# Sparse-attention trunk in split fp32: the key and value compression as split products on token windows, and another order of the attention layer's steps

## The chip, the cores and the metric

The kernel runs on one core of a Trainium2 chip as one launch. The metric is the device time of that launch in microseconds (us); lower is better. Times are medians over several runs. A profile of one further execution gives the trace from which all durations are read. PE is the matmul engine, ACT, DVE and POOL are the three element-wise engines, and SP issues the DMAs of the weights.

## The reference, cut to what matters

The program is a trunk of four layers over 256 tokens of width 1024, all in fp32. Layers 0 and 3 mix tokens by native sparse attention (NSA), layer 1 by block attention (MoBA), layer 2 by a gated convolution; a SwiGLU feed-forward part follows each. The change is in the two NSA layers. There, 16 heads in 4 groups attend in three ways (compressed, selected, window), and a gate weighs the three. What the change touches is the compression of keys and values:

```python
q, k_c, v_c, k_s, v_s, k_w, v_w, gates = jnp.split(h @ w_in, NSA_SPLITS, axis=-1)
n_cmp = (S_ - CMP_BLOCK) // CMP_STRIDE + 1                      # 15 blocks of 32 tokens, 16 apart
cmp_idx = jnp.arange(n_cmp)[:, None] * CMP_STRIDE + jnp.arange(CMP_BLOCK)[None, :]

def compress(kv, pos, w1, w2):
    blk = kv[:, cmp_idx] + pos[None, None, :, None, :]
    blk = jnp.moveaxis(blk, 3, 2).reshape(B_, n_cmp, G, CMP_BLOCK * dh)
    return jax.nn.gelu(blk @ w1) @ w2                            # w1: 2048 x 256, w2: 256 x 64

kc, vc = compress(k_c, pos_k, k_w1, k_w2), compress(v_c, pos_v, v_w1, v_w2)
s_cmp = jnp.einsum('bsgrd,bcgd->bgrsc', q, kc)
o = gates[0] * o_cmp + gates[1] * o_slc + gates[2] * o_win       # (schematic)
```

## The kernel before

**Numbers in halves.** Nearly every product is made of fp32r operands that are split: a high half (the value rounded to fp32r) and a low half (what is left). `mm3` multiplies high by high, high by low and low by high into the same PSUM bank (L200 to L202 when it is called from `group`).

**Weights.** All weights stand in DRAM as one stream of parts. A part is 128 x 1024 fp32 (512 KB), that is 8 tiles of 128 x 128, in the order in which the steps use them: the function `stream` walks the same list of steps. `take` hands out tiles and sees to it that the next five parts are being prepared (`AHEAD`). To prepare a part (`split_part`), SP loads it into a `raw` buffer (6 of them), ACT writes the high half `whi` (L170), and DVE, or POOL where the table `LO` says so, writes the low half `wlo = raw - whi` (L174); `whi` and `wlo` have 5 buffers each. The parts of step F are the exception: SP loads them straight into a `whi` buffer as plain fp32, named `wf`, and nothing is split.

**The NSA layer.** `NSA_ORDER` is a list written by hand; each letter is a step, and the steps' instructions are issued in that order on each engine, as far as a scheduler at build time doesn't interleave neighbours. The steps are:
- A: the raw keys and values for the compression, four projections; `put_raw` copies them, scaled by the row norm, to two tiles `xs`, with a token's place inside its block along the columns.
- K, q, G, V: projections of keys, of query pairs (8 of them), of the gates, and of the values. One of K, q or G is one weight part, 24 matmuls of 128 x 256; V is four parts, 48 matmuls of 128 x 512.
- F (four times, 8 weight parts): `compress`, the product with w1. Before, the weight tile is the stationary operand and a strided view of `xs` with 80 columns (64 blocks and one column for the position's part) the moving one; 64 fp32 matmuls in a layer, all into one PSUM bank (L808).
- E: `activate`, the tanh form of GELU over that bank (L815 on). C and D: the product with w2, for keys and values. c and t: scores and weights of the compressed attention. g: the gates, transposed (L765) and put through a sigmoid.
- s: the scores of one pair of heads (L941, L944) and its softmax: DVE scales and takes the maxima (L587), ACT the exponentials (L591), POOL multiplies by gate and sum (L595). T: transposes of the result (L960 to L962) and its split (ACT L259, DVE L260). P: the product with the values (L979, L984, L986).

After the last P comes the output projection (L220, L224), part of which fills gaps between the last steps. Among the pairs, a stage with little of s, T and P (here called the projection stage) is followed by one in which six of the eight pairs run one after another (the softmax stage).

## Time and profile before

| | before |
|---|---|
| median of 3 runs | 1235.78 us (1235.66 to 1240.07) |
| the profiled execution | 1236.7 us, of it 1234.9 us span |
| PE | 1211.9 us busy (98% of the span) |
| DVE | 959.7 us (78%) |
| ACT | 710.6 us (58%) |
| POOL | 283.2 us (23%) |

Layer 0's attention lies in the first 150 us of the span or so, layer 3's between about 900 and 1040 us. "Busy" is the sum over the records of an engine; matmul records overlap, since a matmul starts before the one ahead of it has ended, so the pace of matmuls is read from the distance of their starts. In the groups of instructions, a row gives source line, engine, operation, what is written from what, the shape, the count, then the busy time, the mean duration in ns, and the engine's idle time ahead with what ended it. In the chain of waits, a row is a start, a length and the work that held the end back.

### The profile page before, as it was taken

To read this page: it belongs to the slowest core of one execution; us is meant where nothing else is said; L and a number is where in the kernel's file an instruction comes from. 1 tells how busy PE (TensorE), PEld (TensorE's weight loads), DVE (VectorE), ACT (ScalarE), POOL (GpSimd) and SP (SyncE) were. 2 spreads that over 40 slices of the span, in tenths; PEclk is the share of its full clock that TensorE was granted. 3 is DMA by queue.
4 is the path that set the end of the run, shared out by engine and by line. 5 is a ranking of instruction groups with operands and counts; after the bars stand their busy time and mean duration, and the time that the engine had idled before them with its cause. 6 is when DMAs were issued, how large, how long until landed. Compare 5 with 4: busy or idle time off the path is not lost.

```text
span 1234.9 us, 19497 instructions
## 1 busy us (share of the span) xinstructions
PE 1211.9 (98%) x6740; PEld 1051.4 (85%) x6740; DVE 959.7 (78%) x1709; ACT 710.6 (58%) x1258; POOL 283.2 (23%) x405
## 2 busy tenths in 40 slices
PE   8999999999999999999999999999999999999997
PEld 8987888888899888888888888888899878888886
DVE  7578798885778797987769897895746787889753
ACT  5489756564456545764444555574435896566543
POOL 1067650010111542000113250000220676400000
PEclk9999999999999999999999999999999999999999
DMA  7773265657555545666765655675768522656671
GB/s 280 249 241 99 69 208 163 221 186 250 191 172 153 172 127 186 233 202 194 278 196 164 191 184 171 200 240 165 245 193 253 157 89 75 221 166 209 198 261 38
DMA packets 96450, 231.40 MB, mean 187 GB/s; under 512 B 18272, under 2 KB 43232, under 8 KB 96352
## 3 DMA queue, kind: packets, MB, share of 16 engines
q1 hardware_dynamic: 95920, 229.61, 57.9%
q8 instruction: 53, 0.87, 0.3%
q10 hardware_dynamic: 432, 0.56, 0.1%
q14 instruction: 45, 0.37, 0.1%
HBM read 213.33 MB, written 1.05 MB: 174 GB/s over the span
## 4 chain that ended last, share of the span: by engine, by line
PE 81%; DVE 7%; ACT 5%; DMA 3%; POOL 2%; issue 1%; SPq 0%; POOLq 0%; ACTq 0%; DVEq 0%
PE psA L220 13%; PE psA L224 7%; PE psA L472 5%; PE psA L470 5%; PE psA L471 5%; PE psB L471 3%; PE psB L472 3%; PE psB L470 3%; PE psA L200 2%; PE psA L202 2%; PE psA L201 2%; DVE wlo L174 2%; PE psB L220 2%; ACT pr L591 2%; PE psB L412 1%; PE psB L410 1%
## 5 line engine op out<-in xcount | busy, mean ns | idle before, releaser
L170 ACT CAST whi<-raw 128x1024 fp32r<-128x1024 f32 (+1 forms) x347 | 357.0, 1038 | 293.6 <-DMA raw<-in_w 54.5
L174 DVE TENSOR_TENSOR wlo<-raw,whi 128x1024 fp32r<-128x1024 f32 (+1 forms) x334 | 410.2, 1246 | 143.9 <-ACT whi L170 121.0
L220 PE MATMUL psA<-ff,whi 128*128 128x512 f32 x686 | 181.8, 392 | 0.1
L220 PEld LDWEIGHTS psA<-ff,whi 128*128 128x128 f32 x686 | 124.6, 189 | 22.8 <-DVE row L1021 0.6
L200 PE MATMUL psA<-at,whi 128*128 128x256 f32 x352 | 101.3, 288 | 1.2 <-DVE row L557 1.2
L595 POOL TENSOR_SCALAR pr<-pr,rc,gates 128x256 f32<-128x256 f32 (+1 forms) x128 | 74.3, 595 | 119.2 <-DVE rc L593 114.5
L224 PE MATMUL psA<-ff,wlo 128*128 128x256 f32 x686 | 101.0, 282 | 0.0
L224 PEld LDWEIGHTS psA<-ff,wlo 128*128 128x128 f32 x686 | 96.0, 191 | 5.4
L202 PE MATMUL psA<-at,wlo 128*128 128x256 f32 x352 | 99.8, 284 | 0.0
L472 PE MATMUL psA<-whi,at 128*128 128x512 f32 x256 | 99.6, 389 | 0.0
L470 PE MATMUL psA<-whi,at 128*128 128x512 f32 x256 | 99.6, 389 | 0.0
L471 PE MATMUL psA<-wlo,at 128*128 128x512 f32 x256 | 99.6, 389 | 0.0
L201 PE MATMUL psA<-at,whi 128*128 128x256 f32 x352 | 99.5, 283 | 0.0
L137 ACT CAST shi<-B 128x1024 fp32r<-128x1024 f32 x56 | 58.8, 1051 | 53.9 <-DVE B L123 21.0
L287 POOL TENSOR_TENSOR ssq<-ssq,row 128x256 f32<-128x256 f32 x42 | 34.1, 811 | 210.6 <-ACT row L285 153.4
L174 POOL TENSOR_TENSOR wlo<-raw,whi 128x256 fp32r<-128x256 f32 x96 | 69.6, 761 | 37.3 <-ACT whi L170 17.3
L138 DVE TENSOR_TENSOR slo<-B,shi 128x1024 fp32r<-128x1024 f32 x56 | 66.7, 1215 | 12.0 <-ACT shi L137 12.0
L471 PE MATMUL psB<-wlo,at 128*128 128x512 f32 x192 | 74.9, 390 | 0.5 <-DVE wlo L174 0.5
L470 PE MATMUL psB<-whi,at 128*128 128x512 f32 x192 | 75.2, 391 | 0.0
L472 PE MATMUL psB<-whi,at 128*128 128x512 f32 x192 | 74.8, 390 | 0.0
L591 ACT ACTIVATE pr<-pr,mn 128x256 f32<-128x256 f32 (+1 forms) x160 | 71.4, 448 | 2.1 <-DVE mn L587 1.4
L200 PEld LDWEIGHTS psA<-at,whi 128*128 128x128 f32 x352 | 67.3, 191 | 1.8 <-ACT whi L170 1.6
(283 smaller groups left out, 2674.3 us busy)
## 6 DMA issues: line engine op xcount, KB each, us to landing
raw<-in_w SPq DMA_DIRECT2D x352, 512.0 KB, 4.5
B<-in_w SPq DMA_DIRECT2D x32, 512.0 KB, 4.2
pt<-pt SPq DMA_DIRECT2D x320, 32.0 KB, 1.9
wf<-in_w SPq DMA_DIRECT2D x16, 512.0 KB, 4.8
keys<-keys SPq DMA_DIRECT2D x16, 128.0 KB, 2.5
ff<-row SPq DMA_DIRECT2D x32, 64.0 KB, 2.9
h<-in_xt SPq DMA_DIRECT2D x4, 256.0 KB, 4.7
raw<-in_w SPq DMA_DIRECT2D x4, 256.0 KB, 5.0
```

The costliest lines, as they stand in the source:

```text
L170: copy(hi[:, c], src[:, c])
L174: eng.tensor_tensor(out=lo[:, d], in0=src[:, d], in1=hi[:, d].bitcast(F32), op=OP.subtract)
L200: mm(out, wt[0], act[0], start=first, stop=False)
L201: mm(out, wt[0], act[1], start=False, stop=False)
L202: mm(out, wt[1], act[0], start=False, stop=last)
L220: mm(outs[o], w[0], acts[k].rearrange("p i s -> p (i s)"), start=(k == 0), stop=(k == n - 1))
L224: mm(outs[o][:, :S], w[1], acts[k][:, 0, :], start=False, stop=False)
L470: mm(o, a[:, 0, s], hi, start=(k == 0), stop=False)
L471: mm(o, a[:, 0, s], lo, start=False, stop=False)
L472: mm(o, a[:, 1, s], hi, start=False, stop=(k == KT - 1))
L591: nc.scalar.activation(pr[:, c], pr[:, c], AF.Exp, bias=mn[:, j:j + 1], scale=-1.0, accum_out=den[:, j:j + 1])
L595: getattr(nc, PR[j % len(PR)]).tensor_scalar(pr[:, c], pr[:, c], rc[:, j:j + 1], gates[j], op0=OP.mult, op1=OP.mult)
```

## The change

Two things change in the NSA layers; all else of the diff gives the same instructions as before (names of unused options, the unused steps O and o, the lists of engines that hold "p" throughout).

First, the order of steps. Second, the compression:
- The parts of F go the common way: `raw` by SP, high half on ACT, low half on DVE (`LO["F"] = "v"`).
- `put_raw` ends, for each of keys and values, in the new function `windows`: four casts of 128 x 256 on ACT and four subtractions of the same shape on DVE write the blocks' tokens as high and low halves side by side (for one place inside a block, 64 columns hold the high halves of 4 groups x 16 blocks, and the next 64 the low ones), and two small pairs of 128 x 16 put the position's part at the sixteenth block, which the compression doesn't use. A layer has twice that.
- `compress` makes these windows the stationary operand and 256 columns of `whi` or `wlo` the moving one: 64 fp32r matmuls of 128 x 256 in a layer into one bank of 512 columns. High and low tokens lie on different partitions of that bank.
- After the last F, ACT and DVE copy the bank's two halves to SBUF, and `activate` begins with 4 fp32 matmuls of 128 x 64 with `fold` (two identities above each other, made once), which add the two halves and turn the result into the layout of before.
- The memsets and copies of the position's part into `xs` go; POOL copies one column of it instead.

The core of the diff:

```diff
-NSA_ORDER = ("A K3 q q F F F K0 F E G g K2 q K1 q D C s c q s V t T q P s T q s P T q T c s s P P T s t P s T "
-             "P T T P P").split()
+NSA_ORDER = ("A G q K0 F q F K2 F F g E q C K1 q q s q c s t T V D s K3 T q P s T P s q T T s P c P s T t P s "
+             "P T T P P").split()
-LO = {"nsa_out": "p", "moba_out": "vp", "A": "p", "F": "ppv"}
+LO = {"nsa_out": "p", "moba_out": "vp", "A": "p", "F": "v"}
...
-        if self.names[q] == "F":
-            t = self.operands.tile([P, PART * P], F32, tag="whi", name=f"wf{q}", bufs=W_BUFS)
-            nc.sync.dma_start(t, self.ap["w"][q])
-            self.parts[x] = (t, t)
-            return
...
-        xs = [self.sb([P, 656], "pt", bufs=PT_BUFS) for _ in range(2)]
+        xs = [self.sb([P, 4, 8, 17], "pt", bufs=PT_BUFS) for _ in range(2)]
+        xw = [[], []]
         for a in range(2):
-            nc.gpsimd.memset(xs[a][:, 512:], 0.0)
-            x = xs[a][:, 512:640].rearrange("p (r c) -> p r c", c=16)
-            for i in range(2):
-                nc.vector.tensor_copy(x[:, :, i], pos[:, a, 8 * i:8 * i + 8])
+            nc.gpsimd.tensor_copy(xs[a][:, :, :, 16], pos[:, a, None, 8:].to_broadcast([P, 4, 8]))
...
+        def windows(a):
+            for hf in range(2):
+                for r in range(0, 8, 4):
+                    x = self.ff([P, 2, S]).rearrange("p i s -> p (i s)").rearrange("p (r i g c) -> p r i g c", r=4, i=2, g=4)
+                    src = xs[a][:, :, r:r + 4, hf:hf + 16].rearrange("p g r c -> p r g c")
+                    nc.scalar.copy(x[:, :, 0], src)
+                    nc.vector.tensor_tensor(out=x[:, :, 1], in0=src, in1=x[:, :, 0].bitcast(F32), op=OP.subtract)
+                    if hf == 0:
+                        src = pos[:, a, r:r + 4, None].to_broadcast([P, 4, 4])
+                        nc.scalar.copy(x[:, :, 0, :, 15], src)
+                        nc.vector.tensor_tensor(out=x[:, :, 1, :, 15], in0=src, in1=x[:, :, 0, :, 15].bitcast(F32),
+                                                op=OP.subtract)
+                    xw[a].append(x.rearrange("p r i g c -> p r (i g c)"))
...
             for jj in range(4 * n, 4 * n + 4):
-                w = self.take(4)[0]
-                for i in range(4):
-                    a, hf = divmod(i, 2)
-                    x = xs[a]
-                    src = bass.AP(tensor=x.tensor, offset=x.offset + jj % 8 * 16 + jj // 8,
-                                  ap=[list(x.ap[0]), [P, 5], [1, 16]])
-                    mm(pc[0][:, 2 * hf + a], w[:, i * P:(i + 1) * P], src, start=(jj == 0 and i == 0),
-                       stop=(jj == 15), skip_group_check=True)
+                hi, lo = self.take(4)
+                for i, w in enumerate((hi, lo)):
+                    for a in range(2):
+                        c = slice(a * S, (a + 1) * S)
+                        mm(pc[0][:, c], xw[a][jj // 4][:, jj % 4], w[:, c], start=(jj == 0 and i == 0 and a == 0),
+                           stop=(jj == 15 and i == 1), skip_group_check=True)
+            if n == 3:
+                halves = [self.row() for _ in range(2)]
+                nc.scalar.copy(halves[0], pc[0][:, :S])
+                nc.vector.tensor_copy(halves[1], pc[0][:, S:])
+                pc.append(halves)
...
+            ph = self.bank("B")
+            for a, x in enumerate(pc[1]):
+                for hf in range(2):
+                    o = (2 * hf + a) * DH
+                    mm(ph[:, o:o + DH], x[:, hf * P:(hf + 1) * P], self.fold, start=(a == 0 and hf == 0), stop=True,
+                       skip_group_check=True)
+            p4 = ph[:, :S].rearrange("p (n c) -> p n c", n=4)
```

What follows shows how this moves instructions. On DVE in layer 0, after the row norm `rb` has come, before; `row` is a projection scaled by the norm, `pt_15` and `pt_16` are the tiles `xs`, and `wlo13` is the low half of weight part 13 (the parts 7 to 12, 14 and 15 are F's and have none):

```order
L729 COPY pt_16_151<-row_39_374 64x128 x2
L729 COPY pt_16_151<-row_40_380 64x128 x2
L557 TENSOR_TENSOR row_41_386<-psA_34_330,rb_36_360 128x256
L557 TENSOR_TENSOR row_44_422<-psA_43_395,rb_36_360 128x256
L748 TENSOR_TENSOR keys_11_144<-row_41_386,keys_11_144 64x256
L748 TENSOR_TENSOR keys_12_145<-row_41_386,keys_12_145 64x256
L781 TENSOR_TENSOR row_45_425<-row_44_422,ff_42_394 128x256
L557 TENSOR_TENSOR row_48_457<-psA_47_430,rb_36_360 128x256
L781 TENSOR_TENSOR row_49_460<-row_48_457,ff_46_429 128x256
L174 TENSOR_TENSOR wlo13_488<-raw13_485,whi13_487 128x1024
L174 TENSOR_TENSOR wlo16_522<-raw16_519,whi16_521 128x1024
```

The same place of the changed program, where L758, L589, L820 and L180 are what L729, L557, L781 and L174 were, L770 and L774 are the windows' large and small subtractions, and `row_49` is the gates' projection:

```order
L758 COPY pt_16_153<-row_44_402 64x8x16 x2
L589 TENSOR_TENSOR row_49_424<-psA_34_332,rb_36_366 128x256
L180 TENSOR_TENSOR wlo9_431<-raw9_428,whi9_430 128x1024
L770 TENSOR_TENSOR ff_45_408<-pt_16_153,ff_45_408 128x4x64
L770 TENSOR_TENSOR ff_46_413<-pt_16_153,ff_46_413 128x4x64
L770 TENSOR_TENSOR ff_47_418<-pt_16_153,ff_47_418 128x4x64
L770 TENSOR_TENSOR ff_48_421<-pt_16_153,ff_48_421 128x4x64
L589 TENSOR_TENSOR row_52_458<-psA_51_427,rb_36_366 128x256
L774 TENSOR_TENSOR ff_45_408<-pos_14_150,ff_45_408 128x4x4
L774 TENSOR_TENSOR ff_46_413<-pos_14_150,ff_46_413 128x4x4
L180 TENSOR_TENSOR wlo10_469<-raw10_466,whi10_468 128x1024
L820 TENSOR_TENSOR row_53_460<-row_52_458,ff_50_426 128x256
```

Between the copies and the first low half that PE needs, DVE had only projections to scale and split; now the windows and the low halves of F's parts stand among them, in one queue.

On PE in layer 0, before, where step F is under way (`wf10`, `wf11` are F's parts, `whi13` and `wlo13` those of K0):

```order
L808 MATMUL psB_50_464<-pt_15_150,wf10_431 128x80 x2
L808 MATMUL psB_50_464<-pt_16_151,wf10_431 128x80 x2
L200 MATMUL psA_51_533<-at_1_118,whi13_487 128x256
L201 MATMUL psA_51_533<-at_1_118,whi13_487 128x256
L808 MATMUL psB_50_464<-pt_15_150,wf11_465 128x80 x2
L808 MATMUL psB_50_464<-pt_16_151,wf11_465 128x80 x2
```

In the changed program, where the first F matmul stands (L840; `ff_39` is a window, `whi9` and `wlo9` belong to the second q, `psB_65` receives the transposed gates):

```order
L207 MATMUL psA_58_534<-at_1_120,whi9_430 128x256
L840 MATMUL psB_56_504<-whi7_202,ff_39_380 128x256
L806 MATMUL psB_65_699<-ident_99,row_49_424 128x128 x2
L208 MATMUL psA_58_534<-at_1_120,wlo9_431 128x256
L206 MATMUL psA_58_534<-at_2_123,whi9_430 128x256
```

F's matmuls and the gates' transposes now stand in PE's queue ahead of a projection, and they read what DVE and ACT write.

On PE in layer 0, before, where the third pair's scores stand (L941 on `ff_61`; the product of the first pair, L979 and L984, is ahead of them):

```order
L202 MATMUL psA_132_1137<-at_8_139,wlo26_1008 128x256
L979 MATMUL psC_135_1178<-pt_128_1127,ff_116_1082 128x512 x2
L979 MATMUL psC_135_1178<-pt_129_1130,ff_118_1088 128x512 x2
L984 MATMUL psC_135_1178<-pt_130_1133,ff_120_1094 128x2x128 x2
L941 MATMUL psA_139_1197<-keys_10_143,ff_61_689 128x256 x4
L944 MATMUL psA_140_1198<-keys_10_143,ff_61_689 128x512 x2
```

The same scores in the changed program (L978 on `ff_70`; L602 to L604 end the values' projection, L892 is step D):

```order
L602 MATMUL psA_125_1106<-whi25_931,at_8_141 128x512
L603 MATMUL psA_125_1106<-wlo25_932,at_8_141 128x512
L604 MATMUL psA_125_1106<-whi25_931,at_8_141 128x512
L978 MATMUL psA_144_1207<-keys_10_145,ff_70_721 128x256 x2
L892 MATMUL psB_134_1179<-w2_13_148,row_135_1180 128x128 x2
L892 MATMUL psB_134_1179<-w2_13_148,row_136_1182 128x128 x2
L892 MATMUL psB_134_1179<-w2_13_148,row_137_1184 128x128 x2
L892 MATMUL psB_134_1179<-w2_13_148,row_138_1186 128x128 x2
L978 MATMUL psA_144_1207<-keys_10_145,ff_70_721 128x256 x2
L981 MATMUL psA_145_1208<-keys_10_145,ff_70_721 128x512 x2
```

The third scores come directly after V; the projection K3 and the first pair's product, which stood ahead of them, now stand behind.

More of the change, by code (lines that the diff above doesn't have):

```diff
@@ L153, in split_part @@
             return
-        if self.names[q] == "F":
-            t = self.operands.tile([P, PART * P], F32, tag="whi", name=f"wf{q}", bufs=W_BUFS)
-            nc.sync.dma_start(t, self.ap["w"][q])
-            self.parts[x] = (t, t)
+        lo_eng, hi_eng = (e.get(self.names[q], d) for e, d in ((LO, "v"), (HI, "a")))
+        lo_eng, hi_eng = (e[q % len(e)] if q >= 4 else d for e, d in ((lo_eng, "v"), (hi_eng, "a")))
+        if lo_eng == "d":
+            hi = self.wp.tile([P, PART * P], F32R, tag="raw", name=f"raw{q}", bufs=RAW_BUFS)
+            lo = self.operands.tile([P, PART * P], F32R, tag="wlo", name=f"wlo{q}", bufs=W_BUFS)
+            nc.gpsimd.dma_start(hi, self.ap["w"][q])
+            nc.scalar.activation(lo, hi.bitcast(F32), AF.Identity, scale=-1.0)
+            nc.gpsimd.dma_start(lo, self.ap["w"][q], accum_op=OP.add)
+            self.parts[x] = (hi, lo)
             return
@@ L331, in project, with open_column, feed_columns, high @@
         self.late = []
+    def open_column(self, acts):
+        self.columns.append([self.bank("A"), [self.take() for _ in range(KT)], 0])
+        self.feed_columns(acts[:-1])
+    def feed_columns(self, acts):
+        mm = self.nc.tensor.matmul
+        for col in self.columns:
+            o, ws, done = col
+            for k in range(done, len(acts)):
+                hi, lo = ws[k]
+                def high():
+                    mm(o, hi, acts[k].rearrange("p i s -> p (i s)"), start=(k == 0), stop=(k == KT - 1))
+                def low():
+                    mm(o[:, :S], lo, acts[k][:, 0, :], start=False, stop=False)
+                for f in (low, high) if k == KT - 1 else (high, low):
+                    f()
+            col[2] = max(done, len(acts))
     def out_proj(self, acts, norm):
         m = 0
-        for n in (4, 1, 1, 1, 1):
-            ps = [self.bank(OUT_BANKS[i]) for i in range(n)]
-            self.group_wide(ps, acts)
+        early, self.columns = self.columns, []
+        for n in ([-len(early)] if early else []) + [4] + [1] * (KT - 4 - len(early)):
+            if n < 0:
+                n = -n
+                self.columns = early
+                self.feed_columns(acts)
+                self.columns = []
+                ps = [c[0] for c in early]
+            else:
+                ps = [self.bank(OUT_BANKS[i]) for i in range(n)]
+                self.group_wide(ps, acts)
             for i, p in enumerate(ps):
@@ L385, in split @@
             def split():
-                with self.tc.issue_after(self.casts.ins), self.tc.issue_after(self.lows.ins):
+                with ExitStack() as behind:
+                    for i in self.latest:
+                        behind.enter_context(self.tc.issue_after(i.ins))
                     halves()
@@ L576, in values, with softmax @@
             put(t, p)
-    def softmax(self, cols, gates):
+    def softmax(self, cols, gates, by):
         nc = self.nc
@@ L650, in project_q @@
             q = self.ff([P, 2, S])
[L651 removed]
+            self.project([lambda x: self.split(q, self.scaled(x))], at)
             qs.append(q)
@@ L884, in compressed @@
             p3 = pc.rearrange("p (h c) -> p h c", c=16)
[L885 to L891 removed]
+            nc.vector.tensor_tensor(out=pc, in0=pq[:, :S], in1=self.cneg, op=OP.add)
             mx = self.sb([P, 16], "cmx")
@@ L1086, in run @@
         nc.vector.memset(self.ones, 1.0)
+        self.fold = const.tile([P, DH], F32, tag="fold", name="fold")
+        nc.gpsimd.tensor_tensor(out=self.fold, in0=self.ident[:, :DH], in1=self.ident[:, DH:], op=OP.add)
         warm = const.tile([P, 1], F32, tag="warm", name="warm")
@@ L1118, in stream @@
     r = lambda a, n: np.arange(a, a + n)
-    out = lambda w, j, step: [(step, w, j, r(0, 512))] + [(step, w, j, r(m * P, P)) for m in range(4, KT)]
+    out = lambda w, j, step, m=0: ([(step, w, j, r(m * P, 512))]
+                                   + [(step, w, j, r(i * P, P)) for i in range(m + 4, KT)])
     s = []
```

98 lines of the change are left out of this document (42 added, 56 removed).

## The prediction

> **What bounds the kernel now.** I began with the page's first part, which tells what each engine was busy with.
>
> ```profile
> span 1234.9 us, 19497 instructions
> ...
> PE 1211.9 (98%) x6740; PEld 1051.4 (85%) x6740; DVE 959.7 (78%) x1709; ACT 710.6 (58%) x1258; POOL 283.2 (23%) x405
> ```
>
> PE is the bound: matmul time that goes away is gained, unless PE then waits. So I cut layer 0's attention and layer 3's into stretches by the table of windows: start and end, length, then busy time (and instructions) of PE, PE's weight loads, DVE, ACT and POOL, the clock, and the share and rate of the DMAs.
>
> ```profile
> 24.00:50.00 26.00, 25.38 (x220) 25.18 (x220) 12.60 (x29) 10.81 (x20) 0.00 (x0) 1.00 0.69 233
> 50.00:86.00 36.00, 34.80 (x241) 31.71 (x240) 29.18 (x85) 26.47 (x62) 14.85 (x20) 1.00 0.77 254
> 86.00:142.00 56.00, 53.15 (x349) 45.45 (x348) 46.33 (x175) 51.18 (x154) 37.48 (x67) 1.00 0.28 83
> 908.00:940.00 32.00, 31.57 (x272) 31.32 (x271) 14.48 (x30) 11.50 (x21) 0.70 (x1) 1.00 0.71 229
> 940.00:960.00 20.00, 20.00 (x166) 19.83 (x166) 17.68 (x48) 14.85 (x34) 1.80 (x2) 1.00 0.82 238
> 960.00:1033.00 73.00, 69.71 (x440) 59.62 (x439) 57.66 (x214) 63.06 (x183) 49.22 (x84) 1.00 0.34 102
> ```
>
> Step F lies in the first row (layer 0) and the fourth (layer 3). There PE is full, and DVE and ACT are idle for more than half of the time. In the third and the last row, the softmax stage, ACT is busy for 91% and 86%, and PE has its idle time: 2.85 and 3.29 us. So the first place is PE's, the second nearly ACT's.
>
> Step F's price stands in the timeline of PE (start, length, what), and its count in the view of line 808:
>
> ```profile
> 921.72 0.28 PE L202 MATMUL psA<-at,wlo 128*128 128x256 f32 x1
> 921.84 9.17 PE L808 MATMUL psB<-pt,wf 128*128 128x80 f32 x80
> 930.81 0.36 PE L200 MATMUL psA<-at,whi 128*128 128x256 f32 x1
> ```
>
> ```profile
> L808 PEld LDWEIGHTS psB<-pt,wf x256: 186/192/193, 29.3 to 939.6; 128*128 128x128 f32 x128
> L808 PE MATMUL psB<-pt,wf x256: 234/274/338, 29.5 to 939.7; 128*128 128x80 f32 x128
> ```
>
> The 80 records from 921.84 to 930.81 come every 0.112 us, and the 128 x 256 matmul ahead of them took its 0.12 us from start to start. The 128 fp32 products of both layers left 256 records, two each: a layer's F costs 128 x 0.112 = 14.3 us.
>
> **F's matmuls.** Now 64 matmuls of 128 x 256 take 64 x 0.12 = 7.7 us, and the 4 fp32 products with `fold`, two records each at 0.112, 0.9 us. A layer's PE work falls by 14.3 - 7.7 - 0.9 = 5.7 us, both by 11.5. Were the new matmuls paced by their weight loads (0.192 us each) instead, F would cost 12.3 us and the gain fall to 1.1 a layer; I don't take it, because the old records, with the same loads, came every 0.112 us.
>
> [...]
>
> **What DVE and ACT get instead.** The prices are in the groups of DVE between 24 and 75 us, and of ACT between 60 and 142 us:
>
> ```profile
> L174 DVE TENSOR_TENSOR wlo<-raw,whi 128x1024 fp32r<-128x1024 f32 x12 | 14.7, 1226 | 9.2 <-ACT whi L170 9.1
> L557 DVE TENSOR_TENSOR row<-psA,rb 128x256 f32<-128x256 f32 x12 | 4.9, 420 | 2.4 <-PE psA L202 2.3
> L748 DVE TENSOR_TENSOR keys<-row,keys 64x256 fp32r<-64x256 f32 x8 | 3.3, 418 | 0.7 <-ACT keys L744 0.5
> L729 DVE COPY pt<-row 64x128 f32<-64x128 f32 x8 | 2.1, 263 | 0.1
> ```
>
> ```profile
> L170 ACT CAST whi<-raw 128x1024 fp32r<-128x1024 f32 x12 | 12.5, 1050 | 4.6 <-PE psA L572 2.0 <-DMA raw<-in_w 1.7 <-ACT ff L929 0.4
> ...
> L779 ACT CAST ff<-row 128x512 fp32r<-128x512 f32 x6 | 3.8, 627 | 1.8 <-DVE row L557 1.8
> L929 ACT ACTIVATE ff<-psA,rstd 128x256 fp32r<-128x256 f32 x8 | 3.7, 480 | 1.5 <-PE psA L572 1.1 <-DVE ff L931 0.4
> ...
> L861 ACT ACTIVATE ff<-gu,rsel 128x512 fp32r<-128x512 f32 x2 | 1.3, 720 | 0.0
> ...
> L744 ACT CAST keys<-row 64x256 fp32r<-64x256 f32 x2 | 0.8, 402 | 0.0
> ```
>
> A layer adds on DVE 8 low halves (9.8 us) and 8 window subtractions (3.4, priced as the 128 x 256 subtraction), and four small ones, for which no row is near: between 0 and 0.26, I take 0.16. That is 13.8 us. ACT gets 8 x 1.05 and 8 x 0.40, 11.6 us.
>
> **The F stretch becomes DVE's.** The new DVE queue from `rb` to the last F part's low half holds ten low halves (12.2), eight scaled projections (3.4), eight copies (2.1), eight windows (3.4), the small ones (0.6), two q and two key halves (1.7) and `rb` (0.4): 23.8 us; before, 10.1 lay between `rb` and the last low half of this stretch. These rows tell when `rb` starts in each layer and when the matmul behind F's last did:
>
> ```profile
> 23.91 0.44 DVE rb L312
> ```
>
> ```profile
> 916.30 0.43 DVE L312 COPY rb<-psB 128x256 f32<-128x256 f32 x1 [4.47 <-PE psB L310]
> ```
>
> ```profile
> 47.41 0.36 PE L200 MATMUL psA<-at,whi 128*128 128x256 f32 x1
> ...
> 90.87 0.63 PE L941 MATMUL psA<-keys,ff 128*128 128x256 f32 x4
> ...
> 141.38 1.17 PE L979 MATMUL psC<-pt,ff 128*128 128x512 f32 x4
> ...
> 939.73 0.36 PE L200 MATMUL psA<-at,whi 128*128 128x256 f32 x1
> ...
> 982.47 0.51 PE L941 MATMUL psA<-keys,ff 128*128 128x256 f32 x3
> ...
> 1032.80 1.17 PE L979 MATMUL psC<-pt,ff 128*128 128x512 f32 x4
> ```
>
> Layer 0: DVE writes F's last low half at 23.9 + 23.8 = 47.7 at the earliest, and PE ends F 0.7 later, at 48.4. By PE alone F would end at 47.4 - 0.6 (the stretch's idle time) - 6.6 (F without `fold`) + 2.9 (five projections stand ahead of F's end instead of four, 24 x 0.12) = 43.1. So PE waits 5.3 us, 4.7 more than before. These waits fall on the gates' transposes (they read a projection that DVE scales only after twelve copies and subtractions), on the first window and on the last low halves; behind them in PE's queue stand q, K2 and all of E. Layer 3: two of the low halves are made ahead of `rb`, so 21.4 us remain; 916.3 + 21.4 + 0.7 = 938.4 against 939.7 - 0.4 - 3.7 = 935.6, a wait of 2.8, 2.4 more. SP's loads of F wait for one of six `raw` buffers now instead of a free `whi`; I give them no price, since a buffer comes free with each low half, 1.2 us apart at best, and the DMAs were busy for 69% and 71% of the stretch.
>
> **The softmax stage starts earlier.** I follow the third pair's scores (L941 at 90.87 and 982.47). Ahead of them, PE loses F's 5.7, K3's 24 matmuls (2.9), the first pair's product (four 128 x 512 and two 128 x 256: 1.2) and D's eight (0.9): 10.7 us. In layer 0 a wait of 1.2 us on V's first projection goes as well:
>
> ```profile
> L200 PE MATMUL psA<-at,whi 128*128 128x256 f32 x48 | 13.9, 289 | 1.2 <-DVE row L557 1.2
> ```
>
> So the scores come at 90.9 - 10.7 + 4.7 - 1.2 = 83.7, 7.2 earlier, and in layer 3 at 982.5 - 10.7 + 2.4 = 974.2, 8.3 earlier. What moved behind them must be done there: on PE 5.2 us more, on ACT, which is the fuller, one weight part (1.05), K3's halves (0.8), two of D's copies (1.4) and two of V's (1.0) more, and one q less (0.6): 3.6 us. I count ACT's growth in full, because its share there is 91%. POOL's gate products keep their order, and the shifts of K3's and the q's rows, which SP issues, come where the DMAs are busy for 28%: no price. The last pair's product (L979 at 141.38 and 1032.80) comes 7.2 - 3.6 = 3.6 us earlier in layer 0 and 8.3 - 3.6 = 4.7 in layer 3. Behind it everything is as before. The sum is 8.3 us.
>
> Bounds: the waits in F could be none (7.1 us more gained) or twice as long (7.1 lost); ACT's growth could cost nothing (7.2 more) or bring three waits of the kind of V's in each layer (7.2 lost). Not all at once: the likeliest case spans 4 to 14 us. The other parts have one answer: four small casts, two copies of the bank's halves and POOL's column lie beside PE work; the unused options add nothing.
>
> The profiled execution took 1236.7, of it 1.8 outside the span, 0.9 above the median. 1236.7 - 8.3 - 0.9 gives 1227.5 us (own range 1222 to 1232).
>
> **Rivals.** *ACT keeps its idle time.* From the first scores to the last split, ACT's sum by these prices is the same in both orders, 69 us; ACT idles 9.5 us of the 36 in the second window, partly on V's matmuls. If V holds it up as long as before, the end moves only with the first scores. Ahead of these PE loses 5.3 us (F's 5.7, while C's 0.4 comes ahead of them), less the waits of 4.7 and 2.4: 0.6 and 2.9 us, 1232.3 in all. For it: V's 10.9 us stand in one piece still. Against: its idle time is there because T, q and P follow V before new scores come, and these now go elsewhere.
>
> *All of the work is gained.* DVE fills its idle time ahead of `rb`, PE loses no more in F than before, and the softmax stage gives up its idle 2.85 + 3.29 us: 11.5 + 6.1 = 17.6, 1218.2 us. Against: the sum of 23.8 us after `rb` can't begin before the projections are scaled.
>
> *Slower: DVE is held up by ACT's casts in the F stretch.* Low halves wait for the cast of their part: DVE's row says 9.1 us of idle time behind ACT's casts in 51 us. If 7.8 of these come on top of the 23.8 us, because casts queue behind the windows' casts and these behind DVE's scaling, each layer loses 7.8: 1227.5 + 15.6 = 1243.1. It decides from 4.2 us of such idle time a layer on, where the gain is gone. Against: ACT adds up to under half of the stretch, and today's idle time is that of a queue with nothing to do.
>
> *The halves don't pace at 0.12:* with the loads' 0.192, the gain falls by 4.6 a layer, to 1236.7.
>
> **Numbers.** Forecast 0.55; ACT's idle time 0.22; all gained 0.13; slower 0.07; pace 0.03. About 0.5%, 6.2 us, is what a measurement of this kernel can tell from no change: below 1229.6 counts as faster, above 1242.0 as slower. Of the forecast's range three quarters are faster: 0.41 + 0.13 = 0.54; slower 0.07 and 0.01 from the tails, 0.08; the rest is 0.38. The range runs from 1219 (most of "all gained" left out) to 1238 (slower left out).
>
> **What would show it.** Right: L840 every 0.12 us, 7.7 us a layer; DVE busy for over 90% from `rb` to F's end, at about 48 and 938 us; PE's idle time there on L806, L840 and low halves, 3 to 6 us; the third scores at about 84; ACT over 90% behind them. Wrong: F ending at 43 (DVE has room), ACT casts as DVE's releaser for over 4 us (the slower rival), or the third scores early and the last product not (ACT's idle time).

## The result, and the profile after the change

The changed kernel takes 1230.69 us (median of 6 runs, 1228.91 to 1232.4), the kernel before 1236.82 (6 runs, 1235.66 to 1240.07): a ratio of 0.9949, 95% interval 0.9934 to 0.9964. It is 6.1 us faster; 8.3 were forecast. In executions of the kernel before with a mean granted clock of 0.998 or more it took 1236 to 1239 us, in those with 0.996 or less 1240 to 1243, so its medians, and the ratios to it, depend on how many of either kind stand beside a run. The changed kernel's profiled execution took 1231.72, 1.0 above its median, with this first part of the page:

```profile
span 1229.9 us, 19380 instructions
...
PE 1202.0 (98%) x6628; PEld 1043.2 (85%) x6628; DVE 985.2 (80%) x1743; ACT 732.5 (60%) x1300; POOL 288.0 (23%) x406
```

PE is as full as before, with 9.9 us less busy time; DVE has 25.5 us more and ACT 21.9. The table of windows shows where the gain lies. The stretches of layer 0 are now cut at four events: the copy of `rb`, the end of step F, the third pair's scores and the last pair's product (layer 3 likewise; the fourth row runs from the last product to the next layer's `rb`). Before:

```profile
23.91:47.41 23.50, 22.88 (x201) 22.68 (x199) 10.37 (x25) 10.24 (x18) 0.00 (x0) 1.00 0.67 232
...
90.87:141.38 50.51, 47.74 (x311) 40.52 (x310) 42.99 (x167) 46.06 (x145) 33.33 (x61) 1.00 0.26 81
141.38:351.63 210.25, 210.03 (x1051) 178.63 (x1051) 168.44 (x219) 113.64 (x152) 38.25 (x46) 1.00 0.61 197
916.30:939.73 23.43, 23.00 (x201) 22.75 (x199) 12.82 (x28) 11.40 (x19) 0.00 (x0) 1.00 0.70 220
...
982.47:1032.80 50.33, 47.48 (x312) 40.55 (x310) 42.83 (x167) 46.05 (x145) 33.50 (x61) 1.00 0.27 81
```

And after:

```profile
23.70:48.92 25.22, 22.59 (x163) 21.82 (x162) 23.15 (x46) 19.25 (x37) 0.00 (x0) 0.86 0.63 186
48.92:83.19 34.27, 34.19 (x232) 30.95 (x231) 30.61 (x87) 26.06 (x62) 15.21 (x19) 1.00 0.84 282
83.19:138.26 55.07, 51.16 (x351) 45.26 (x350) 48.00 (x178) 51.53 (x154) 37.87 (x67) 1.00 0.30 92
138.26:349.12 210.86, 210.86 (x1056) 179.67 (x1056) 168.53 (x219) 113.61 (x152) 38.09 (x46) 1.00 0.60 196
913.82:934.99 21.17, 19.94 (x163) 19.30 (x162) 20.45 (x43) 18.79 (x36) 0.00 (x0) 1.00 0.55 171
934.99:972.05 37.06, 34.97 (x232) 31.13 (x231) 30.81 (x88) 27.52 (x65) 15.13 (x19) 1.00 0.78 258
972.05:1027.13 55.08, 51.19 (x352) 45.30 (x350) 48.01 (x178) 51.53 (x154) 37.87 (x67) 1.00 0.27 87
```

From `rb` to the third scores the time fell from 66.96 to 59.49 us in layer 0 and from 66.17 to 58.23 in layer 3: 7.5 and 7.9 earlier. The softmax stage took 4.6 and 4.75 of that back: 50.51 and 50.33 before, 55.07 and 55.08 now. ACT's busy time in it rose from 46.06 to 51.53.

Busy time says little about an engine that is at 98%, because a busy PE can also be a PE with a slower pace (below, 0.21 us between the starts of matmuls of 128 x 256 instead of 0.12). For the comparisons below I split the length of each stretch into PE's work and the rest. The work is the count of its matmul records by their undisturbed pace: 0.112 us up to 128 columns (the prediction's row for 80; transposes of 128 from 87.07 to 87.62 us start 0.11 apart) and 0.12 for 256 (its rows), and 0.2275 for 512 (0.227 between starts from 198.97 to 203.96 us). With the last, the stretch from 138.26 to 349.12, which PE fills, comes out at 786 x 0.2275 + 259 x 0.12 + 10 x 0.112 = 211.0 of its 210.86 us. What is left of a length is waiting, or matmuls at a lower clock. The starts of F's last matmul and of the scores and products are the cuts:

| work + rest, us | `rb` to last F | to third scores | softmax stage | to the next `rb`, or the end | whole |
|---|---|---|---|---|---|
| before, layer 0 | 22.6 + 0.8 | 41.5 + 2.0 | 44.4 + 6.1 | 209.9 + 0.4 | 318.4 + 9.3 |
| after, layer 0 | 19.1 + 6.0 | 33.5 + 0.9 | 49.1 + 6.0 | 211.0 - 0.2 | 312.7 + 12.7 |
| before, layer 3 | 22.6 + 0.7 | 41.5 + 1.3 | 44.4 + 5.9 | 195.5 + 6.6 | 304.1 + 14.6 |
| after, layer 3 | 19.1 + 2.0 | 33.5 + 3.7 | 49.1 + 6.0 | 196.6 + 6.1 | 298.3 + 17.8 |

The whole work falls by 5.7 us in each layer, as forecast for F, and the rest grows by 3.4 and 3.2 us. So the profiled execution gains 2.3 and 2.5 us (327.73 to 325.42, 318.62 to 316.08), which is nearly all of the span's 5.0.

F's new matmuls run at the pace that was taken from the projections. PE's timeline in layer 0:

```profile
40.27 0.40 PE L840 MATMUL psB<-whi,ff 128*128 128x256 f32 x2
40.52 0.40 PE L840 MATMUL psB<-wlo,ff 128*128 128x256 f32 x2
```

Two in 0.25 us, 0.12 each. F's stretch has become DVE's: it is busy for 23.15 of 25.22 us and for 20.45 of 21.17, where it had 10.37 and 12.82. Its groups between `rb` and F's end:

```profile
L180 DVE TENSOR_TENSOR wlo<-raw,whi 128x1024 fp32r<-128x1024 f32 x12 | 14.5, 1220 | 0.7 <-ACT whi L176 0.7
L770 DVE TENSOR_TENSOR ff<-pt,ff 128x256 fp32r<-128x256 f32 x8 | 2.9, 418 | 0.0
```

In layer 0 PE does not only wait there. Its timeline, with the idle time ahead of an instruction and its releaser in brackets:

```profile
30.16 0.35 PE L840 MATMUL psB<-whi,ff 128*128 128x256 f32 x1 [0.52 <-DVE ff L774]
32.18 0.69 PE L806 MATMUL psB<-ident,row 128*128 128x128 f32 x2 [1.67 <-DVE row L589]
33.31 0.58 PE L208 MATMUL psA<-at,wlo 128*128 128x256 f32 x1 [0.44 <-DVE wlo L180]
...
36.26 0.41 PE L206 MATMUL psA<-at,whi 128*128 128x256 f32 x1
36.47 0.41 PE L207 MATMUL psA<-at,whi 128*128 128x256 f32 x1
```

The first window, the gates' transposes and a low half hold PE up for 2.6 us within 3.7, and behind them its matmuls come 0.21 us apart instead of 0.12. The table of windows gives the reason in its clock column, the third from the right:

```profile
32.00:34.00 2.00, 1.37 (x5) 0.97 (x6) 2.00 (x5) 2.00 (x6) 0.00 (x0) 0.51 0.00 0
34.00:36.00 2.00, 2.00 (x11) 2.00 (x11) 1.78 (x6) 1.87 (x6) 0.00 (x0) 0.50 0.82 240
36.00:38.00 2.00, 2.00 (x12) 2.00 (x11) 2.00 (x4) 0.01 (x1) 0.00 (x0) 0.50 0.49 88
38.00:39.00 1.00, 1.00 (x7) 1.00 (x7) 0.39 (x1) 1.00 (x1) 0.00 (x0) 0.58 0.59 209
```

A window counts every matmul that reaches into it, so these counts overlap. By their starts, 24 matmuls begin between 34 and 39, 2.9 us of work at 0.12: PE is shown busy all the time and loses 2.1 us. From the low half at 33.31 on it is 2.5 us, nearly as much as the three waits together. From 39 on they come at 0.12 again, as the rows of L840 above show. In layer 3 the clock stays whole.

### The profile page after: what moved, and what is told of

The parts are those of the page before. It is cut to its first block, busy times and chain, and to the rows that moved or that the text cites. A ratio compares the mean times of both kernels' runs of the same rounds, so it can differ in the third digit from the quotient of the medians.

```text
span 1229.9 us, 19380 instructions
## 1 busy us (share of the span) xinstructions
PE 1202.0 (98%) x6628; PEld 1043.2 (85%) x6628; DVE 985.2 (80%) x1743; ACT 732.5 (60%) x1300; POOL 288.0 (23%) x406
## 3 DMA queue, kind: packets, MB, share of 16 engines
HBM read 213.33 MB, written 1.05 MB: 174 GB/s over the span
## 4 chain that ended last, share of the span: by engine, by line
PE 83%; ACT 6%; DVE 5%; issue 2%; DMA 2%; POOL 1%; SPq 0%; POOLq 0%; ACTq 0%; DVEq 0%
PE psA L226 13%; PE psA L230 7%; PE psA L504 5%; PE psA L502 5%; PE psA L503 5%; PE psB L502 4%; PE psB L504 4%; PE psB L503 4%; ACT pr L622 3%; PE psA L208 2%; PE psA L206 2%; PE psA L207 2%; PE psB L226 2%; DVE wlo L180 2%; PE psB L444 1%
## 5 line engine op out<-in xcount | busy, mean ns | idle before, releaser
L176 ACT CAST whi<-raw 128x1024 fp32r<-128x1024 f32 (+1 forms) x363 | 373.3, 1039 | 289.6 <-DMA raw<-in_w 55.8
L180 DVE TENSOR_TENSOR wlo<-raw,whi 128x1024 fp32r<-128x1024 f32 (+1 forms) x350 | 428.3, 1241 | 130.1 <-ACT whi L176 106.4
L626 POOL TENSOR_SCALAR pr<-pr,rc,gates 128x256 f32<-128x256 f32 (+1 forms) x128 | 76.9, 614 | 111.3 <-DVE rc L624 109.4
L180 POOL TENSOR_TENSOR wlo<-raw,whi 128x256 fp32r<-128x256 f32 x96 | 70.4, 767 | 34.7 <-issue 17.4
L622 ACT ACTIVATE pr<-pr,mn 128x128 f32<-128x128 f32 (+1 forms) x160 | 71.2, 448 | 2.4 <-DVE mn L619 1.7
```

The costliest lines, as they stand in the source:

```text
L176: copy(hi[:, c], src[:, c])
L180: eng.tensor_tensor(out=lo[:, d], in0=src[:, d], in1=hi[:, d].bitcast(F32), op=OP.subtract)
L622: nc.scalar.activation(pr[:, c], pr[:, c], AF.Exp, bias=mn[:, j:j + 1], scale=-1.0, accum_out=den[:, j:j + 1])
L626: {"p": nc.gpsimd, "v": nc.vector}[by[j % len(by)]].tensor_scalar(pr[:, c], pr[:, c], rc[:, j:j + 1], gates[j], op0=OP.mult, op1=OP.mult)
```

## The experiments

The theory was that three things share out F's 5.7 us a layer: DVE's queue and the halved clock in F's stretch, and the work that the new order brings into the softmax stage. The rivals were that one part of the change does it all (the new F, or the order), that the wait for windows and gates decides and not DVE's sum, and, for the stage, that one engine alone sets its length (PE by its moved matmuls, ACT or DVE by their sums).

**Each part alone.** The new F with the old order:

```diff
-NSA_ORDER = ("A G q K0 F q F K2 F F g E q C K1 q q s q c s t T V D s K3 T q P s T P s q T T s P c P s T t P s "
+NSA_ORDER = ("A K3 q q F F F K0 F E G g K2 q K1 q D C s c q s V t T q P s T q s P T q T c s s P P T s t P s T "
```

> The new compression in the old order of steps. Theory 1 (the gain is F's PE work, but only the new order gives DVE the time to make F's halves): F's three steps in a row find DVE with 13.8 us more to do and fewer projections beside it, so PE waits for nearly all of the 5.7 us that F saves in each layer; 1233 to 1237 us. Theory 2 (the new compression alone does it, the order is neutral): 1230 to 1231.5 us. Theory 3 (the order alone does it): 1236 to 1238 us, with F's end no earlier than before.

It took 1238.76 us beside 1237.38 of before, ratio 1.0005 (0.9994 to 1.0016). The old F with the new order, in the kernel before, is the same line changed the other way:

```diff
-NSA_ORDER = ("A K3 q q F F F K0 F E G g K2 q K1 q D C s c q s V t T q P s T q s P T q T c s s P P T s t P s T "
+NSA_ORDER = ("A G q K0 F q F K2 F F g E q C K1 q q s q c s t T V D s K3 T q P s T P s q T T s P c P s T t P s "
```

> The old fp32 compression in the new order of steps. Theory 1 (the gain is F's PE work): the third scores come about 5 us earlier in each layer, since K3, the first pair's product and D no longer stand ahead of them, but the softmax stage has that work added and gives it back; 1235 to 1238 us. Theory 3 (the order alone does it): 1230 to 1232 us.

It took 1237.55, ratio 0.9993 (0.9979 to 1.0006). So neither part gains anything by itself. With the new F alone, all of the 5.7 us of work is saved in each layer (312.7 and 298.3) and the rest grows to 16.8 and 20.8 us, with PE waiting for the windows' subtractions in one piece. Its timeline, in layer 0 and in layer 3:

```profile
34.92 0.58 PE L840 MATMUL psB<-whi,ff 128*128 128x256 f32 x1 [4.23 <-DVE ff L774]
...
927.01 0.39 PE L840 MATMUL psB<-whi,ff 128*128 128x256 f32 x1 [3.30 <-DVE ff L774]
```

With the new order alone, F's stretch and the next lose their waits (in layer 0 the rest there is -0.1 and 0.0 us, 2.8 before), and the softmax stage takes it back. Its two stages in the table of windows:

```profile
80.05:140.65 60.60, 53.30 (x363) 46.06 (x361) 51.25 (x181) 53.98 (x160) 40.49 (x69) 1.00 0.32 97
977.92:1032.71 54.79, 49.64 (x336) 43.21 (x335) 46.38 (x176) 50.50 (x152) 36.92 (x65) 1.00 0.28 82
```

The order spreads F's parts among other steps, so that DVE's new work has cover; the new F pays. That the gain needs both is shown.

**F's stretch: who sets it.** First, POOL makes half of F's low halves, in four pieces each:

```diff
-LO = {"nsa_out": "p", "moba_out": "vp", "A": "p", "F": "v"}
+LO = {"nsa_out": "p", "moba_out": "vp", "A": "p", "F": "vp"}
```

> The changed kernel with every second low half of F's parts on POOL, which does nothing in that stretch: DVE's sum there falls by 4 x 1.22 = 4.9 us. If DVE is what bounds the F stretch: in layer 0 PE's waits of 2.6 us and the time at half clock behind them shrink, F ends 2 to 4 us earlier, and a good part of it arrives at the end; 1225 to 1229 us. If not (PE waits for something else, or POOL, at 4 x 0.77 us a part and beside DVE's subtractions, is later than DVE was): 1230 to 1234 us, F's end where it is or later.

1235.54 us, ratio 0.9976 (0.9963 to 0.9988): better than before, worse than the change. F ends no earlier: its last matmul starts 25.46 and 24.98 us after `rb` in layers 0 and 3, 25.10 and 21.04 in the changed kernel (F's end is told by this start in all the runs that follow). POOL's timeline, and then PE's:

```profile
35.38 12.79 POOL L180 TENSOR_TENSOR wlo<-raw,whi 128x256 fp32r<-128x256 f32 x12 [10.08 <-ACT whi L176]
```

```profile
48.22 0.39 PE L840 MATMUL psB<-wlo,ff 128*128 128x256 f32 x1 [0.49 <-POOL wlo L180]
```

POOL needs 12.8 us in a row for three low halves that DVE makes in 3.7, PE waits for it at F's end, and DVE's own get longer beside it:

```profile
36.31 1.44 DVE L180 TENSOR_TENSOR wlo<-raw,whi 128x1024 fp32r<-128x1024 f32 x1
39.54 1.64 DVE L180 TENSOR_TENSOR wlo<-raw,whi 128x1024 fp32r<-128x1024 f32 x1
```

The four low halves that begin while POOL is at work took 1.33 to 1.64 us, against 1.22 in the changed kernel, where POOL does nothing there. This run moved the bound to POOL and so doesn't tell what a lighter DVE would give.

Next, the windows of one of the two tiles `xs` are subtracted by POOL, which takes four large and two small subtractions from DVE, 4 x 0.42 + 2 x 0.19 = 2.1 us:

```diff
+            eng = nc.vector if a else nc.gpsimd
...
-                    nc.vector.tensor_tensor(out=x[:, :, 1], in0=src, in1=x[:, :, 0].bitcast(F32), op=OP.subtract)
+                    eng.tensor_tensor(out=x[:, :, 1], in0=src, in1=x[:, :, 0].bitcast(F32), op=OP.subtract)
...
-                        nc.vector.tensor_tensor(out=x[:, :, 1, :, 15], in0=src, in1=x[:, :, 0, :, 15].bitcast(F32),
+                        eng.tensor_tensor(out=x[:, :, 1, :, 15], in0=src, in1=x[:, :, 0, :, 15].bitcast(F32),
```

> The changed kernel with the windows' subtractions for the keys on POOL, those for the values still on DVE: DVE has 2.0 us less to do between the row norm and the last window, which PE now sees at 35.4 us. If the chain from the row norm to the last window makes PE's waits in layer 0 (2.6 us, and the half clock behind them): the last window comes 1.5 to 2 us earlier, the clock stays whole, layer 0 gains 2 to 4 us, layer 3 under 1 us; 1226 to 1229 us. If the last low halves bound the stretch, or POOL and DVE hold each other up: F's end as it is, 1230 to 1233 us.

1229.03 us, ratio 0.9932 (0.9908 to 0.9957): no different from the changed kernel. In the profiled execution (1231.88) F ends at 24.98 after `rb` in layer 0, 0.1 earlier, though DVE has less to do, and at 21.78 in layer 3, 0.7 later. The wait has gone to POOL, and the clock is halved all the same; PE's timeline, and the window:

```profile
31.41 0.38 PE L841 MATMUL psB<-whi,ff 128*128 128x256 f32 x1 [1.60 <-POOL ff L775]
```

```profile
34.00:39.00 5.00, 5.00 (x25) 5.00 (x25) 4.35 (x10) 3.50 (x9) 0.00 (x0) 0.51 0.76 226
```

Then the waits were moved in one piece, with the gates' projection behind the third F:

```diff
-NSA_ORDER = ("A G q K0 F q F K2 F F g E q C K1 q q s q c s t T V D s K3 T q P s T P s q T T s P c P s T t P s "
+NSA_ORDER = ("A q K0 F q F K2 F G F g E q C K1 q q s q c s t T V D s K3 T q P s T P s q T T s P c P s T t P s "
```

> The changed kernel with the gates' projection (G) behind F's third step instead of second in the list, so that their transposes no longer stand in PE's queue behind the first F matmul. If the waits of 1.67 us on the transposes are what drops PE's clock to half from 32 to 38.6 us in layer 0: the clock stays at 1.00 there; F's end moves little (DVE's sum is the same), 0.5 to 1.5 us; 1229 to 1230.5 us. If the half clock itself costs its whole 3.3 us: 1227 to 1228 us. If PE only waits elsewhere: clock and time as in the changed kernel, 1230.7 us.

1235.98 us, ratio 0.998 (0.9969 to 0.9991): less than half of the change's gain. The gates no longer hold PE up there, but between the first tile's window (a matmul at 30.44) and the second tile's PE now has two matmuls to do, and waits:

```profile
35.25 0.58 PE L840 MATMUL psB<-whi,ff 128*128 128x256 f32 x1 [4.23 <-DVE ff L774]
```

```profile
34.00:39.00 5.00, 3.75 (x17) 3.75 (x18) 3.81 (x10) 4.24 (x10) 0.00 (x0) 0.50 0.48 136
```

So what the changed kernel does between the two tiles, the gates' transposes and a q's projection, is cover for the windows, and the transposes' wait of 1.67 us is the smaller price. With all of F behind K2, PE has 48 more matmuls ahead of the first window:

```diff
-NSA_ORDER = ("A G q K0 F q F K2 F F g E q C K1 q q s q c s t T V D s K3 T q P s T P s q T T s P c P s T t P s "
+NSA_ORDER = ("A G q K0 q K2 F F F F g E q C K1 q q s q c s t T V D s K3 T q P s T P s q T T s P c P s T t P s "
```

> The changed kernel with all four F steps behind G, q, K0, q and K2, so that PE has 14 us of projections to do while the windows are made. If the waits for windows and gates, and the half clock that follows them, are what the F stretch loses (4 to 6 us in layer 0, under 1 us in layer 3): no such wait, clock 1.00, F ends at 46 to 47 us instead of 48.9 in layer 0 and about where it is in layer 3; 1227 to 1229 us. If DVE's low halves bound it all the same (8 x 1.22 us for 7.7 us of F): PE waits on them instead, F's end stays, 1230 to 1232 us.

1229.66 us, ratio 0.9936 (0.9913 to 0.996). In layer 0 there is no wait for windows or gates left, and the clock is whole. What PE waits for now is one low half after the other:

```profile
38.85 0.50 PE L840 MATMUL psB<-wlo,ff 128*128 128x256 f32 x2 [0.70 <-DVE wlo L180]
41.22 0.50 PE L840 MATMUL psB<-wlo,ff 128*128 128x256 f32 x2 [1.04 <-DVE wlo L180]
```

```profile
34.00:39.00 5.00, 4.30 (x34) 3.85 (x33) 4.63 (x11) 4.95 (x10) 0.00 (x0) 1.00 0.63 156
```

These waits are 3.2 us in all. F ends 24.23 us after `rb` in layer 0, 0.9 earlier, and 22.18 in layer 3, 1.1 later: without the first waits and with the whole clock, DVE's queue of low halves holds PE up nearly as long, which is the prediction's reading of the stretch. Against the changed kernel that is too little to measure. Both edits together (this order, and the half of the windows on POOL as above):

```diff
-NSA_ORDER = ("A G q K0 F q F K2 F F g E q C K1 q q s q c s t T V D s K3 T q P s T P s q T T s P c P s T t P s "
+NSA_ORDER = ("A G q K0 q K2 F F F F g E q C K1 q q s q c s t T V D s K3 T q P s T P s q T T s P c P s T t P s "
...
+            eng = nc.vector if a else nc.gpsimd
```

> All four F steps behind K2, and the windows' subtractions for the keys on POOL. With F behind K2, PE waited 3.2 us in layer 0 and 1.2 us in layer 3 on low halves by DVE. If DVE's sum is what makes them late: DVE has 2.0 us less ahead of them, and F ends 1 to 2 us earlier in layer 0 and up to 1 in layer 3; 1 to 3 us faster than with F behind K2 alone, 7 to 10 us under the kernel before. If DVE and POOL hold each other up, or the casts on ACT are late instead: as with F behind K2 alone.

1230.08 us, ratio 0.9925 (0.9905 to 0.9945). F ends at 23.81, another 0.4 earlier, but the next stretch gives that back: its rest in layer 0 is 2.3 us instead of 1.2, among it a wait of `fold` for ACT's copy:

```profile
50.16 0.66 PE L855 MATMUL psB<-fold,row 128*128 128x64 f32 x4 [0.94 <-ACT row L845]
```

What the clock itself costs was tried by filling the gap: 20 more matmuls of 128 x 256 ahead of layer 0's first F matmul, into the bank that it then starts.

```diff
+                for k in range(20 if j == 0 else 0):
+                    mm(pc[0][:, :S], at[k % KT][:, 0, :P], at[k % KT][:, 1, :], start=True, stop=True, skip_group_check=True)
```

> The changed kernel with 20 more matmuls of 128 x 256 (2.4 us, their result is overwritten) ahead of the first F matmul of layer 0 alone, where PE waits for 2.6 us in all. If the half clock from 32 to 38.6 us comes from those waits and costs what it slows (PE does half the work in 6.6 us): the clock stays at 1.00, the second q and the first F steps run 2 to 3 us faster, F ends 0.5 to 1.5 us earlier where the low halves allow it, and the whole is 0.5 to 1.5 us faster than the changed kernel on the same chip, though it does more work. If the half clock has another cause: it stays, and the whole is equal or up to 2.4 us slower.

1231.07 us, ratio 0.9936 (0.9912 to 0.9959). The clock stays whole and F ends at 23.01 after `rb`, 2.1 us earlier, with 2.4 us more work on PE. Still no gain is seen in total, and the third scores come 0.9 later. The two windows, ACT's timeline and PE's show why:

```profile
34.00:39.00 5.00, 4.96 (x42) 4.76 (x41) 4.77 (x11) 4.56 (x10) 0.00 (x0) 1.00 0.60 150
...
44.00:50.00 6.00, 4.32 (x36) 4.11 (x35) 4.26 (x5) 2.87 (x5) 0.00 (x0) 1.00 0.98 291
```

```profile
48.13 1.05 ACT L176 CAST whi<-raw 128x1024 fp32r<-128x1024 f32 x1 [2.07 <-DMA raw<-in_w]
```

```profile
49.23 0.39 PE L206 MATMUL psA<-at,whi 128*128 128x256 f32 x1 [1.68 <-ACT whi L176]
```

PE waits 1.68 us for a high half, and ACT had waited 2.07 for the weights, with the DMAs busy for 98%. In this run the loading of weights stands behind the halved clock. So the clock's loss is real in its stretch, and taking it away brought no measurable gain in the end. What it costs the changed kernel over all its executions isn't shown.

How long the halving lasts isn't set by the waits alone. It lasted 6.83 us in the changed kernel and in its repeat, and 3.41 in three runs below that change nothing ahead of F and have nearly the same three waits (D early, K3 early, D's copies on DVE). There F ended 24.1 to 24.2 us after `rb`, 0.9 to 1.0 earlier than in the changed kernel: as much as the order with F behind K2 brought.

**The softmax stage: who sets it.** Step D goes back ahead of the stage:

```diff
-NSA_ORDER = ("A G q K0 F q F K2 F F g E q C K1 q q s q c s t T V D s K3 T q P s T P s q T T s P c P s T t P s "
+NSA_ORDER = ("A G q K0 F q F K2 F F g E q C K1 q D q s q c s t T V s K3 T q P s T P s q T T s P c P s T t P s "
```

> The changed kernel with D ahead of the first scores, where the old order had it, instead of ahead of the third. It takes out of the softmax stage (third scores to last product, 55.1 us in the changed kernel, 50.5 before) 0.9 us of PE, 1.8 us of ACT and about 2.6 us of DVE, and puts them ahead of it, where PE pays 0.9. If ACT's sum sets the stage's length: 53.3 us, in all 1229 us. If DVE's: 52.5 us, in all 1227.5 us. If PE's work does: 54.2 us and nothing gained, 1230.7 us.

1234.38 us beside 1237.21 of before, ratio 0.9975 (0.9961 to 0.9989): worse than the change. The stage gets 1.45 us shorter, the scores come 3.0 us later in layer 0 and 1.6 in layer 3 (62.5 and 59.8 after `rb`). K3 ahead of the stage:

```diff
-NSA_ORDER = ("A G q K0 F q F K2 F F g E q C K1 q q s q c s t T V D s K3 T q P s T P s q T T s P c P s T t P s "
+NSA_ORDER = ("A G q K0 F q F K2 F F g E q C K1 q q K3 s q c s t T V D s T q P s T P s q T T s P c P s T t P s "
```

> The changed kernel with K3 ahead of the first scores instead of behind the third: the softmax stage loses 2.9 us of PE, 1.9 us of ACT and 2.5 us of DVE, and the scores come about 2.9 us later. If ACT's sum sets the stage's length: 53.2 us instead of 55.1, in all 1 us a layer slower than the changed kernel. If PE's work does: 52.2 us, as fast as the changed kernel. If DVE's: 52.6 us. If none of them, but a chain through all: 55 us, 2.9 us a layer slower.

1236.43 us, ratio 0.9979 (0.9966 to 0.9992). The stage in the table of windows, first with D early, then with K3 early:

```profile
86.45:140.07 53.62, 49.74 (x335) 43.57 (x334) 46.21 (x175) 49.91 (x152) 37.01 (x65) 1.00 0.30 90
```

```profile
84.84:140.35 55.51, 50.92 (x324) 43.11 (x323) 46.67 (x175) 50.00 (x151) 36.11 (x66) 0.97 0.29 96
```

Against the changed kernel, K3 early takes 3.6 us of PE's work out of the stage (49.1 to 45.5), 1.5 of ACT's and 1.3 of DVE's, and the stage is 0.4 longer (0.1 in layer 3). But the clock in its row is 0.97. Inside the stage lies a stretch with a halved clock, and another like it in layer 3 (1003.60 to 1007.01):

```profile
112.72:116.13 3.41, 3.41 (x18) 3.12 (x17) 2.44 (x10) 3.23 (x11) 1.51 (x4) 0.50 0.21 72
```

In it 15 matmuls begin, 1.8 us of work by the paces above, so about 1.6 us are the clock's. Without them the stage would take an estimated 53.9 us, 1.2 less than in the changed kernel. By PE's sum alone it would be 3.6 less, which doesn't fit; ACT's 1.5 or DVE's 1.3 would fit, so this run does not rule those out. That it came near the number expected for a chain through all of them is partly the clock's doing.

Over before, the change, these two and the new order alone, the stage is longer than ACT's busy time by 3.5 to 6.6 us, than DVE's by 7.1 to 9.4 and than PE's work by 6.0 to 10.8. The 6.6 is from layer 0 of the new order alone, at the whole clock; so no single engine's sum gives the length in all of these orders. What sets it in the changed one stays open.

To take work off ACT alone, DVE makes all four copies of step D's values, of which ACT makes two (0.72 us each):

```diff
-OWN = "vava"
+OWN = "vvvv"
```

> The changed kernel with D's four selected copies all on DVE, two of which were on ACT: in the softmax stage ACT has 1.4 us less, DVE 1.0 us more, PE the same. If ACT's sum sets the stage's length: 53.6 us instead of 55.1, in all 1228 us. If DVE's: 56.1 us, 1232.5 us. If PE's work, or a chain through all of them: 55.1 us, 1230.7 us.

1237.81 us, ratio 1.0 (0.9983 to 1.0017). It tells nothing of ACT, because the order on POOL changed with it. POOL's timeline, and then PE's:

```profile
105.30 2.83 POOL L180 TENSOR_TENSOR wlo<-raw,whi 128x256 fp32r<-128x256 f32 x4 [0.80 <-ACT whi L176]
108.12 4.11 POOL L626 TENSOR_SCALAR pr<-pr,rc,gates 128x128 f32<-128x128 f32 x8
```

```profile
128.07 0.73 PE L226 MATMUL psA<-ff,whi 128*128 128x512 f32 x2 [2.45 <-DVE mn L619]
```

A low half of 2.83 us now stands ahead of the products with the gates, and PE waits 2.45 us later on: the stage takes 58.34. The clock is halved in it too, for 3.41 us from 111.82 and from 128.89, and once in layer 3's stage. Inconclusive.

**The change once more.** Without an edit, beside the last kernels, to see what two profiles of one kernel differ by:

> The changed kernel itself once more, for a comparison on the same chip as the three that follow: 0.9934 to 0.9964 of the kernel before, as the first time; the third scores to the last product take 55.1 us in both layers, and the clock of PE falls to half somewhere between 30 and 39 us.

1230.49 us beside 1237.83, ratio 0.9929 (0.9908 to 0.995); span 1228.3. The two layers take 325.07 and 314.82, so 0.35 and 1.26 less than in the first profile: differences of a us between two kernels' profiles say nothing. The kernels with the windows half on POOL, with F behind K2 and with both lie 0.4 to 1.7 us under the two medians of the changed one, too little to tell them from it. Five runs (the new F alone, half of the low halves on POOL, the gates late, D early, D's copies on DVE) came out slower than every value that was expected of them. No version was found that surely beats it.

## Why the prediction came out as it did

The sign, the size within its range and most of the steps were right. One step was mis-sized and a smaller one was wrong; these two make up the difference between 8.3 us and the 4.9 that the two layers gained in the profiled execution. In a third step the number was met partly by luck.

- *F's matmuls.* Right: 0.12 us each, and PE's work falls by 5.7 us in each layer in every kernel with the new F.
- *The F stretch becomes DVE's.* Right in its direction; in layer 0 the size is partly luck. Forecast: F's end (the start of the matmul behind it) at 48.4 in layer 0 and 22.1 us after `rb` in layer 3; measured 48.9 and 21.2. DVE is busy for 92% and 97%. PE's rest grew by 5.2 and 1.3 us (forecast 4.7 and 2.4). But in layer 0 PE waited for only 2.6 us where the prediction has 5.3, and not at all for the last low halves; about 2.5 us are a thing that the prediction did not have, the halved clock. With the clock whole F ended 0.9 (F behind K2) to 2.1 us (gap filled) earlier, and the layer gained at most 0.8: DVE's low halves, or the weights, are the next bound.
- *The third scores.* Right: 7.5 and 7.9 us earlier, forecast 7.2 and 8.3.
- *The softmax stage.* This step failed in size: "I count ACT's growth in full", 3.6 us. The stage grew by 4.6 and 4.75, ACT's busy time by 5.5: the list was too short. ACT's groups in the stage, after and then before, name what was missed:

```profile
L265 ACT CAST pt<-psB 128x512 fp32r<-128x512 f32 x22 | 12.1, 590 | 1.3 <-PE psB L998 1.1
...
L966 ACT ACTIVATE ff<-psA,rstd 128x256 fp32r<-128x256 f32 x6 | 2.7, 478 | 0.0
...
L896 ACT CAST gu<-psB 128x256 fp32r<-128x256 f32 x1 | 0.4, 399 | 0.0
```

```profile
L259 ACT CAST pt<-psB 128x512 fp32r<-128x512 f32 x21 | 11.4, 591 | 1.5 <-PE psB L961 1.3
...
L929 ACT ACTIVATE ff<-psA,rstd 128x256 fp32r<-128x256 f32 x3 | 1.4, 470 | 0.4 <-DVE ff L931 0.4
```

  One transposed part of the probabilities more (0.6), D's cast (0.4) and three activations of V instead of two (0.3 more) make 1.3 of the missing 1.9 us; the rest is at the stretch's edges, in the casts of weights (3.4 us of them lay inside before, 5.5 now, where one of 1.05 more was counted). Of the 5.5, ACT took 0.9 from its idle time (4.45 to 3.54). PE's moved work, 4.7 us ("5.2 us more" by the prediction, whose three items make 5.0), would have given the same growth, with PE's rest the same, 6.1 us before and 6.0 after. The run with K3 early doesn't fit PE's sum alone, and its halved clock keeps it from deciding more, so that ACT sets the length is argued and not shown.
- *"Behind it everything is as before."* Wrong by 0.6 us a layer. Five matmuls of 128 x 512 of the output projection, 27 before and 22 now, no longer fit ahead of the last product; 5 x 0.2275 = 1.1 us are done behind it, and 0.5 of that in time that was idle.

Of the 3.4 us between the forecast and the profile, these two terms are 2.1 and 1.3. The rival that ACT keeps its idle time (3.5 us in all, 1232.3) came nearer by its number: the measured 1230.69 lies between the two. Its mechanism was half right. By it the end moves only as far as the first scores do; these come 2.4 us earlier behind `rb` in layer 3 (35.7 after it, 38.1 before), where 2.5 were gained, but 0.3 in layer 0 (38.0, 38.3), where 2.3 were. The rivals "all of the work is gained", "DVE is held up by ACT's casts" (DVE's low halves waited 0.7 us for them, against 7.8) and "the halves don't pace" are refuted by the rows above.

There is a shorter way to the number. PE is the bound on both sides, so moved matmuls can't gain, only those that go: 5.7 a layer, less the growth of PE's rest (its waits and its time at a halved clock). K3, D and the first product, 5 us that the prediction counted as a gain ahead of the third scores, had to come back behind them; what it left to find was the growth of the rest, 3.4 and 3.2 us.

What stays open is what sets the length of the softmax stage. Moving D did not tell the engines apart, moving K3 brought a halved clock into the stage, and the run meant to unload ACT changed something else besides.

## What to carry to other kernels

Where one engine is at 98%, count the work that goes away and the growth of that engine's waits; work that only moves past a mark is not a gain, and the forecast for the mark behind it has to get it back in full. When an engine receives work from the bound engine, follow its queue from the event that feeds it to the matmul that needs its last result, as DVE's 23.8 us here: in layer 0, F's last matmul started 22.98 us behind the row norm at the earliest, whatever the edit. And look at the clock inside a stretch before you put its length down to waits.
